# Expert slots in four column quarters instead of two halves in a two-layer hybrid diffusion backbone

## The chip, the cores and the metric

The kernel runs on one core of a Trainium2 chip. The metric is the device time of one execution in microseconds, as the median of three runs. All arithmetic of the part that is changed is in fp32.

## The reference

Two layers, each a mixer (differential attention beside a Mamba-2 scan) and an expert-choice mixture of experts. There are 512 latent rows and 256 context rows of 1024 columns. Only the mixture of experts is touched. Each of 16 experts picks its best rows: 64 latent ones, and in layer 0 also 32 context ones. The second layer has no context output.

```python
def expert_choice_ffn(h, w_router, w_gate, w_up, w_down):
    b, n, d = h.shape
    cap = EC_CAPACITY * n // N_EXPERTS
    aff = jax.nn.softmax(jnp.einsum("bnd,de->ben", h, w_router).astype(jnp.float32), axis=1)
    gate, idx = lax.top_k(aff, cap)
    xe = jax.vmap(lambda hb, ib: hb[ib])(h, idx)
    hid = jax.nn.silu(jnp.einsum("becd,edf->becf", xe, w_gate)) * jnp.einsum("becd,edf->becf", xe, w_up)
    ye = jnp.einsum("becf,efd->becd", hid, w_down) * gate[..., None].astype(h.dtype)
    return jax.vmap(lambda ib, yb: jnp.zeros((n, d), yb.dtype).at[ib.reshape(-1)].add(yb.reshape(-1, d)))(idx, ye)
```

The inner width is 1408, that is 11 blocks of 128. An expert's weights are 8 row blocks (k) of w_gate and w_up, 704 KB each, and 11 blocks of w_down, 512 KB each: 17 MB per expert and layer.

## The kernel before

The method `moe` runs the 16 experts of a layer one after the other. For the latent slots (`lat`, L1489), the chosen rows stand transposed in xeT and are the stationary operand; the weights stream past them. The 64 slots fill half of the array's 128 columns, so two matmuls stand side by side (j = 0, 1), each taking one half of every 128 inner columns. Their result gl has partitions (j, slot) and is held in three tiles of 512, 512 and 384 columns, gate and up side by side. `act` turns each into SiLU(gate) times up (ScalarE's Tanh, then two operations on VectorE), into lh. `turned` (L1537) transposes lh back by matmuls with the identity, into hlt, and ScalarE copies that into hl, where the inner columns lie on the partitions. The down projection yl (L1623) again has two halves, 512 output columns each.

For the context slots of layer 0 (`con`, L1573), 32 slots fill a quarter of the columns, so four matmuls stand side by side. Their result gc goes through `act`, and VectorE transposes it in blocks of 32 by 32 (L1619) into hc. The down projection yc (L1581) has four quarters of 256 output columns.

`add_rows` (L1663, L1664) weighs the result by the gate and by the layer's modulation G2 on VectorE into ys. A DMA issued by POOL adds the rows of ys to xr, xc or out in memory, at the addresses in sidx. A latent row is added in two pieces of 512 columns (2 KB), a context row in four of 256 (1 KB).

The sync engine (SP) issues all weight loads in the order of the program: w_gate and w_up of the 8 k, then the 11 blocks of w_down. There are 9 buffers gw, 8 of a ring rt and 6 wd, so a load waits for the buffer that an earlier matmul frees. Each DMA that adds to xr or out also waits for the one before it on the same tensor. In layer 0, `following` (called at the eighth block of yl) transposes the next expert's rows (xet) and gathers those of the one after. In layer 1, `pick` takes them from SBUF by matmuls (slp, xpk, xet).

A scheduler orders each engine's instructions by its own estimate, except where `manual_schedule` keeps the order of the code. Before, that is the case for TensorE in layer 0's last expert alone.

One fp32 matmul has two records in the trace: 48 matmuls of gl per expert are 96 records.

Of the kernel before, what the change touches and what calls it, by code (L numbers as in the profile page):

```python
# [8 lines left out]
F32 = mybir.dt.float32  # L9
# [133 lines left out]
class Net:  # L143
# [122 lines left out]
    def consts(self, p1):  # L266
# [5 lines left out]
        self.twice = cst.tile([64, P], F32, name="twice")  # L272
# [11 lines left out]
        for j in range(2):  # L284
            self.lds(self.twice[:, 64 * j:64 * j + 64], I["k_ident"][0:64, 0:64])
# [1074 lines left out]
    def route_b(self, l, psp):  # L1360
# [25 lines left out]
        ps = psp.tile([P, 2, NE], F32, tag="tr", name="sgp", bufs=3)  # L1386
        nc.tensor.matmul(ps.rearrange("p i e -> p (i e)"), self.twice, c.rearrange("p i e -> p (i e)"), start=True, stop=True)
        nc.vector.tensor_scalar(self.gate[:, 0], ps[:, 0], 0.5, None, op0=OP.mult)
        for j in range(2):
            h = slice(64 * j, 64 * j + 64)  # L1390
            nc.vector.tensor_scalar(self.sidx[h, 0], ps[h, 1], 2.0, 2.0 * P * na + j, op0=OP.mult, op1=OP.add)
# [10 lines left out]
    def route_d(self, l, psp):  # L1402
# [17 lines left out]
        nc.vector.tensor_scalar(self.gate[:, 1], ps[:, 0], 0.5, None, op0=OP.mult)  # L1420
        nc.vector.tensor_copy(self.sidx[:, 1], ps[:, 1])
# [62 lines left out]
    def lat(self, gl, k, c):  # L1484

        a, b = FB[c]
        for j in range(2):
            w = self.ws[k].rearrange("p u (t j i) -> p j u t i", j=2, i=64)[:, j, :, a:b]
            self.nc.tensor.matmul(gl[c][64 * j:64 * j + 64, 0:LW[c]].rearrange("p (u t i) -> p u t i", u=2, i=64), self.xT[:, k, 0:64],  # L1489
                                  w, start=k == 0, stop=k == KD - 1, skip_group_check=True)  # L1490

    def gl_tiles(self):
        return [self.scp.tile([P, 512], F32, tag="L", name="gl", bufs=3) for _ in LW]

# [7 lines left out]
    def moe_open(self, l):  # L1502
# [3 lines left out]
        self.G2 = [mw.tile([P, 512 >> s], F32, name="G2" + "lc"[s]) for s in range(2 if ctx else 1)]  # L1506
# [3 lines left out]
    def G2_load(self, l, s, o):  # L1510

        m = 2 << s
        w, q = D // m, P // m
        for j in range(m):
            self.ld(o[q * j:q * j + q], self.modd[l, s:s + 1, 5 * D + w * j:5 * D + w * j + w].to_broadcast([q, w]))

    def moe(self, l):
# [4 lines left out]
        dst = [b.rearrange("n (j c) -> (n j) c", c=512 >> i) for i, b in enumerate(base)]  # L1522
        mw, G2 = self.mw, self.G2
        def act(h, g, u, n, tag):
            th = mw.tile([P, n], F32, tag=tag + "th", name="th", bufs=2)
            nc.scalar.activation(th, g, AF.Tanh, scale=0.5)  # L1526
# [3 lines left out]
        def turned(o, h, c):  # L1530

            a, b = FB[c]
            tr = psp.tile([P, 4, 64], F32, tag="tr", name="hlt", bufs=3)
            for t in range(a, b):
                for j in range(2):
                    p = slice(64 * j, 64 * j + 64)
                    nc.tensor.matmul(tr[p, t - a], h[:, 64 * t:64 * t + 64], self.ident[:, p], start=True, stop=True, skip_group_check=True)  # L1537
            nc.scalar.copy(o[:, a:b], tr[:, 0:b - a])

        xe = None  # L1540
        for e in range(NE):
# [19 lines left out]
            hl = mw.tile([P, NF, 64], F32, tag="hl", name="hl", bufs=1)  # L1561
            h = mw.tile([P, 704], F32, tag="lh", name="lh", bufs=1)
# [13 lines left out]
            def down(e, hc, wd):  # L1576

                y = psp.tile([P, 512], F32, tag="acc", name="yc")[:, 0:256]
                for b in range(NF):
                    for j in range(4):  # L1580
                        nc.tensor.matmul(y[32 * j:32 * j + 32], hc[:, b], wd[b][:, 256 * j:256 * j + 256],  # L1581
                                         start=b == 0, stop=b == NF - 1, skip_group_check=True)
                if last:
                    self.tail = lambda: self.add_last(y, e, dst)
                else:
                    self.add_rows(mw, y, 1, e, G2, dst)

            with self.tc.manual_schedule(engines={mybir.EngineType.PE}) if last else contextlib.nullcontext():
                turn = iter(range(KD) if ctx else ())

                def cons(n):
                    for k in itertools.islice(turn, n):
                        con(k)

                KB = KD - 2
                for k in range(0 if early else KB):
                    for c in range(3):
                        self.lat(gl, k, c)
                    cons(not last)
                for c in range(3):  # L1600
                    for k in range(KD if early else KB, KD):
                        self.lat(gl, k, c)
                    n = LW[c] // 2
                    act(h[:, 256 * c:256 * c + n], gl[c][:, 0:n], gl[c][:, n:2 * n], n, f"l{c // 2}")
# [281 lines left out]
```

## Time and profile before

| | us |
|---|---|
| median of 3 runs | 2473.05 (2472.52 to 2476.19) |
| the profiled execution | 2473.73 |
| its span, first to last instruction | 2471.9 |
| TensorE busy (matmuls) | 2262.0, 92% |
| VectorE, ScalarE, POOL busy | 956.8, 669.7, 430.8 |
| layer 0's experts, from the first gl to the last yc | about 560 to 1355 |
| layer 1's experts | about 1819 to 2472 |

The page's first part has the busy times. A busy TensorE need not run at its best rate, so the durations of groups count more than the share. The windows show for any stretch what each engine did, the granted clock of TensorE (1.00 is 2.4 GHz) and the share of the 16 DMA engines; that share can exceed 1 slightly, as packets overlap. The timeline merges equal neighbours: a row says when a group began, how long it ran to the end of its last one, and how many records it has. Matmuls overlap at their ends, so the time that a group takes is read from its start to the next group's start.

### The profile page before, as it was taken

The numbers are of one execution on the slowest core, as the hardware profiler recorded it, in microseconds if no ns is written. First come the engines' busy times: TensorE is split into PE (matmuls) and PEld (weight loads), VectorE is DVE, ScalarE is ACT, GpSimd is POOL, SyncE is SP. The second block draws the span as 40 slices with busy tenths as digits, with TensorE's granted clock in tenths as the row PEclk, the third lists the DMA queues.
The fourth block names the chain that finished last, engine by engine and source line by source line (L and its number), as shares of the span: only waits on it lengthen the run. The fifth ranks groups of instructions, "written<-read, shape, count | busy, mean of one in ns | idle before, by whom it ended". The sixth has DMA issues, their size and how long they took to land.

```text
span 2471.9 us, 39924 instructions
## 1 busy us (share of the span) xinstructions
PE 2262.0 (92%) x15496; PEld 1255.7 (51%) x15496; DVE 956.8 (39%) x2924; ACT 669.7 (27%) x1835; POOL 430.8 (17%) x554
## 2 busy tenths in 40 slices
PE   6898988999999999999998888998979998888887
PEld 4777777774333333333333667787735533333332
DVE  5789588772011101110011888778731010101010
ACT  4344557422112111211111434555311110111110
POOL 4454333000000100010001364433000000000000
PEclk9999999999999999999999999999989999999999
DMA  7223722589999999999995322614699999999998
GB/s 251 84 75 111 254 57 94 193 292 341 401 402 384 360 374 373 355 359 364 377 364 162 102 82 88 207 59 149 226 377 412 412 416 412 416 413 416 412 417 317
DMA packets 230088, 701.73 MB, mean 284 GB/s; under 512 B 30316, under 2 KB 79452, under 8 KB 229900
## 3 DMA queue, kind: packets, MB, share of 16 engines
q1 hardware_dynamic: 220364, 681.69, 71.3%
q0 software_dynamic: 9536, 17.49, 3.6%
q8 instruction: 123, 2.02, 0.3%
q14 instruction: 65, 0.53, 0.1%
HBM read 675.34 MB, written 23.76 MB: 283 GB/s over the span
## 4 chain that ended last, share of the span: by engine, by line
PE 57%; DMA 18%; DVE 16%; issue 4%; ACT 3%; POOL 1%; SPq 0%; POOLq 0%; ACTq 0%; DVEq 0%
PE gl L1489 17%; PE yl L1623 10%; PE gc L1573 7%; DMA gw<-w_up 6%; DMA gw<-w_gate 5%; PE pacc L172 4%; PE yc L1581 4%; PE oacc L172 3%; DMA rt<-w_down 3%; DMA wd<-w_down 2%; PE xacc L172 1%; DVE nm L1798 1%; PE hlt L1537 1%; PE po L1827 1%; DVE G L1076 1%
## 5 line engine op out<-in xcount | busy, mean ns | idle before, releaser
L1489 PE MATMUL gl<-gw,xeT 128*64 128x512 f32 (+1 forms) x3072 | 669.0, 569 | 56.2 <-DMA gw<-w_up 52.2
L1489 PEld LDWEIGHTS gl<-gw,xeT 128*64 128x64 f32 x3072 | 249.2, 138 | 451.2 <-issue 412.5
L1623 PE MATMUL yl<-rt,hl 128*64 128x512 f32 x1020 | 279.8, 599 | 0.2
L1527 DVE SCALAR_TENSOR_TENSOR th<-th,gl 128x256 f32<-128x256 f32 (+1 forms) x96 | 38.1, 397 | 459.7 <-ACT th L1526 459.7
L172 PE MATMUL pacc<-rt,H 128*128 128x384 f32 (+1 forms) x768 | 204.7, 348 | 4.3 <-ACT V L1717 2.0
L1573 PE MATMUL gc<-gw,xeT 128*32 128x352 f32 x2048 | 181.8, 464 | 0.0
L1526 ACT ACTIVATE th<-gl 128x256 f32<-128x256 f32 (+1 forms) x96 | 35.1, 366 | 531.5 <-PE gl L1489 519.1
L1663 DVE SCALAR_TENSOR_TENSOR ys<-yl,gate,G2l 128x512 f32<-128x512 f32 x32 | 24.0, 751 | 375.8 <-PE yl L1623 375.8
L1664 POOL DMA_INDIRECT out<-ys,sidx x16 | 24.8, 1550 | 723.7 <-DVE ys L1663 723.7
L172 PEld LDWEIGHTS pacc<-rt,H 128*128 128x128 f32 x768 | 136.3, 195 | 17.4 <-issue 6.3
L172 PE MATMUL xacc<-H,rt 128*128 128x512 f32 (+1 forms) x448 | 135.8, 379 | 7.1 <-ACT H L803 6.6
L1527 DVE SCALAR_TENSOR_TENSOR th<-th,gc 128x352 f32<-128x352 f32 x16 | 8.3, 520 | 324.0 <-ACT th L1526 324.0
L172 PE MATMUL pacc<-rt,L 128*128 128x384 f32 (+1 forms) x384 | 129.2, 336 | 0.0
L1623 PEld LDWEIGHTS yl<-rt,hl 128*64 128x64 f32 x1020 | 71.6, 136 | 98.6 <-issue 90.8
L1429 POOL DMA_INDIRECT xe<-xn2d,gidx x16 | 15.1, 943 | 610.9 <-PE xet L1439 491.5
L1526 ACT ACTIVATE th<-gc 128x352 f32<-128x352 f32 x16 | 7.4, 463 | 406.8 <-PE gc L1573 406.8
L138 POOL TENSOR_TENSOR rt<-raw,rt 128x384 fp32r<-128x384 f32 (+1 forms) x88 | 100.2, 1163 | 92.0 <-ACT rt L130 90.7
L1573 PEld LDWEIGHTS gc<-gw,xeT 128*32 128x32 f32 x2048 | 57.0, 109 | 106.1 <-issue 102.5
L1623 PE MATMUL yl<-wd,hl 128*64 128x512 f32 x388 | 108.8, 604 | 0.6 <-DMA wd<-w_down 0.5
L172 PE MATMUL oacc<-woh,mT 128*128 128x512 f32 x304 | 107.3, 410 | 0.0
L172 PEld LDWEIGHTS xacc<-H,rt 128*128 128x128 f32 x448 | 82.7, 198 | 22.6 <-ACT H L803 7.4
L1803 ACT ACTIVATE e<-sc,nm,rq 128x768 f32<-128x768 f32 (+1 forms) x80 | 72.0, 903 | 54.3 <-DVE nm L1799 50.1
(411 smaller groups left out, 3643.3 us busy)
## 6 DMA issues: line engine op xcount, KB each, us to landing
gw<-w_gate SPq DMA_DIRECT2D x256, 704.0 KB
gw<-w_up SPq DMA_DIRECT2D x256, 704.0 KB
rt<-w_down SPq DMA_DIRECT2D x255, 512.0 KB
wd<-w_down SPq DMA_DIRECT2D x97, 512.0 KB
mr<-w_mod SPq DMA_DIRECT2D x80, 512.0 KB
raw<-w_in SPq DMA_DIRECT2D x48, 256.0 KB
raw<-w_in SPq DMA_DIRECT2D x64, 192.0 KB
RB<-acsd SPq DMA_DIRECT2D x20, 512.0 KB
```

Source lines behind the costliest of these rows:

```text
L138: e.tensor_tensor(lo.bitcast(F32R), x, hi, op=OP.subtract)
L172: self.nc.tensor.matmul(o, a[x].bitcast(F32R), b[y].bitcast(F32R), start=start and i == 0, stop=stop and i == 2, **kw)
L1076: nc.vector.scalar_tensor_tensor(E[:, h], cbm[:, 1], d[:, 1, h:h + 1], E[:, h], op0=OP.mult, op1=OP.add)
L1489: self.nc.tensor.matmul(gl[c][64 * j:64 * j + 64, 0:LW[c]].rearrange("p (u t i) -> p u t i", u=2, i=64), self.xT[:, k, 0:64], w, start=k = ...
L1526: nc.scalar.activation(th, g, AF.Tanh, scale=0.5)
L1527: nc.vector.scalar_tensor_tensor(th, th, 1.0, g, op0=OP.add, op1=OP.mult)
L1537: nc.tensor.matmul(tr[p, t - a], h[:, 64 * t:64 * t + 64], self.ident[:, p], start=True, stop=True, skip_group_check=True)
L1573: nc.tensor.matmul(gc[u][32 * j:32 * j + 32].rearrange("p (t i) -> p t i", i=32), xT[:, k, 64:96], w, start=k == 0, stop=k == KD - 1, skip ...
L1581: nc.tensor.matmul(y[32 * j:32 * j + 32], hc[:, b], wd[b][:, 256 * j:256 * j + 256], start=b == 0, stop=b == NF - 1, skip_group_check=True)
L1623: nc.tensor.matmul(y[64 * j:64 * j + 64], hl[:, b], wd[b][:, 512 * j:512 * j + 512], start=b == 0, stop=b == NF - 1, skip_group_check=True)
L1664: nc.gpsimd.indirect_dma_start(out=dst[i], out_offset=bass.IndirectOffsetOnAxis(ap=self.sidx[:, i, e:e + 1], axis=0), in_=ys, in_offset=No ...
L1803: nc.scalar.activation(ei[:, 0:w], sc[:, i * w:i * w + w], AF.Exp, scale=rq[:, t, i:i + 1], bias=nm[:, i:i + 1], accum_out=sm[:, i:i + 1])
```

## The change

All slots go in groups of 32. The 64 latent slots are two groups g, and for each group four matmuls stand side by side, one per quarter of the inner (or output) columns. The inner columns of blocks 0 to 7 are one gl tile per group; blocks 8 to 10 of both groups share the third. VectorE transposes h in blocks of 32 by 32, as it did for the context; `turned` and its matmuls are gone. Latent rows are added in four pieces of 256 columns, one DMA per group. The order of TensorE is written out for all experts of layer 0 but the first, and in it yc follows yl from the fifth block on. The gate and address tables get a third column, and are spread over the quarters by eight small matmuls (sgp) instead of one.

```diff
-FB = ((0, 4), (4, 8), (8, 11))
+FA = 8
...
     def lat(self, gl, k, c):
-        a, b = FB[c]
-        for j in range(2):
-            w = self.ws[k].rearrange("p u (t j i) -> p j u t i", j=2, i=64)[:, j, :, a:b]
-            self.nc.tensor.matmul(gl[c][64 * j:64 * j + 64, 0:LW[c]].rearrange("p (u t i) -> p u t i", u=2, i=64), self.xT[:, k, 0:64],
-                                  w, start=k == 0, stop=k == KD - 1, skip_group_check=True)
+        w = self.ws[k].rearrange("p u (t j i) -> p j u t i", j=4, i=32)
+        for g, (a, b), o in (((c, (0, FA), 0),) if c < 2 else ((0, (FA, NF), 0), (1, (FA, NF), 192))):
+            n = 64 * (b - a)
+            for j in range(4):
+                self.nc.tensor.matmul(gl[c][32 * j:32 * j + 32, o:o + n].rearrange("p (u t i) -> p u t i", u=2, i=32),
+                                      self.xT[:, k, 32 * g:32 * g + 32], w[:, j, :, a:b], start=k == o == 0, stop=k == KD - 1,
+                                      skip_group_check=True)
...
-        def turned(o, h, c):
-            a, b = FB[c]
-            tr = psp.tile([P, 4, 64], F32, tag="tr", name="hlt", bufs=3)
-            for t in range(a, b):
-                for j in range(2):
-                    p = slice(64 * j, 64 * j + 64)
-                    nc.tensor.matmul(tr[p, t - a], h[:, 64 * t:64 * t + 64], self.ident[:, p], start=True, stop=True, skip_group_check=True)
-            nc.scalar.copy(o[:, a:b], tr[:, 0:b - a])
+        def down(y, h, wd, b, new=True):
+            for j in range(4):
+                nc.tensor.matmul(y[32 * j:32 * j + 32], h[:, b], wd[b][:, 256 * j:256 * j + 256],
+                                 start=new and b == 0, stop=b == NF - 1, skip_group_check=True)
...
+            def lat_act(c):
+                if c < 2:
+                    act(h[:, c, 0:256], gl[c][:, 0:256], gl[c][:, 256:512], 256, "l0")
+                    nc.vector.transpose(hl[:, c, 0:FA].rearrange("p t s -> p (t s)"), h[:, c, 0:256])
+                    return
+                v = gl[2][:, 0:384].rearrange("p (x u i) -> p x u i", x=2, u=2)
+                act(h[:, :, 256:FQ], v[:, :, 0], v[:, :, 1], 192, "l2")
+                for g in range(2):
+                    nc.vector.transpose(hl[:, g, FA:NF].rearrange("p t s -> p (t s)"), h[:, g, 256:FQ])
...
-            with self.tc.manual_schedule(engines={mybir.EngineType.PE}) if last else contextlib.nullcontext():
+            with self.tc.manual_schedule(engines={mybir.EngineType.PE}) if ctx and e else contextlib.nullcontext():
...
-                turned(hl, h, 0)
-                cons(not last)
-                turned(hl, h, 1)
+                if ctx and not last:
+                    for k in range(0 if early else KB, KD):
+                        con(k)
+                    yc = con_act()
                 y = self.scp.tile([P, 512], F32, tag="L", name="yl", bufs=3)
                 for b in range(NF):
-                    if b == 4:
-                        turned(hl, h, 2)
-                        if ctx and not last:
-                            act(h2, gc[0], gc[1], FQ, "c")
-                            nc.vector.transpose(hc.rearrange("p t s -> p (t s)"), h2)
+                    for g in range(2):
+                        down(y[:, 256 * g:256 * g + 256], hl[:, g], wd, b, g == 0)
+                    if ctx and not last and b > 3:
+                        for i in range(5) if b == 4 else (b,):
+                            down(yc, hc, wd, i)
                     if b == 7 and e + 1 < NE:
                         xe = self.following(l, e, xe, nt)
-                    for j in range(2):
-                        nc.tensor.matmul(y[64 * j:64 * j + 64], hl[:, b], wd[b][:, 512 * j:512 * j + 512],
-                                         start=b == 0, stop=b == NF - 1, skip_group_check=True)
-                self.add_rows(mw, y, 0, e, G2, dst)
+                for g in range(2):
+                    self.add_rows(mw, y[:, 256 * g:256 * g + 256], g, e, G2[0], dst[0])
...
-        ys = mw.tile([P, 512 >> i], F32, tag=f"ys{i}", name="ys", bufs=2)
+        ys = mw.tile([P, 256], F32, tag="ys", name="ys", bufs=4)
```

TensorE's order in layer 0 from the end of an expert's main loop, before (the fifteenth expert; gl and gc are the projections, hlt the transposes, yl and yc the down projections, xet the next expert's rows):

```order
L1489 MATMUL gl<-gw,xeT 64x512 x4
L1489 MATMUL gl<-gw,xeT 64x384 x2
L1573 MATMUL gc<-gw,xeT 32x352 x8
L1489 MATMUL gl<-gw,xeT 64x512 x4
L1489 MATMUL gl<-gw,xeT 64x384 x2
L1537 MATMUL hlt<-ident,lh 64x64 x8
L1573 MATMUL gc<-gw,xeT 32x352 x4
L1537 MATMUL hlt<-ident,lh 64x64 x8
L1623 MATMUL yl<-rt,hl 64x512 x8
L1537 MATMUL hlt<-ident,lh 64x64 x6
```

The same place of the changed kernel:

```order
L1490 MATMUL gl<-gw,xeT 32x512 x8
L1490 MATMUL gl<-gw,xeT 32x192 x8
L1573 MATMUL gc<-gw,xeT 32x352 x8
L1490 MATMUL gl<-gw,xeT 32x512 x16
L1490 MATMUL gl<-gw,xeT 32x192 x16
L1573 MATMUL gc<-gw,xeT 32x352 x16
L1536 MATMUL yl<-rt,hl 32x256 x40
L1536 MATMUL yc<-rt,hc 32x256 x20
```

Before, gl is 64 columns wide and gc 32, and hlt stands ahead of yl; now every matmul here is 32 wide, and gl's last two k, gc's last two and five blocks of yl follow each other with nothing between.

TensorE's order in the down projection of the same expert, before:

```order
L1623 MATMUL yl<-rt,hl 64x512 x2
L1439 MATMUL xet<-ident,xe 128x96 x5
L1623 MATMUL yl<-rt,hl 64x512 x2
L1439 MATMUL xet<-ident,xe 128x96 x3
L1581 MATMUL yc<-rt,hc 32x256
L1623 MATMUL yl<-rt,hl 64x512 x2
L1581 MATMUL yc<-rt,hc 32x256 x8
L1623 MATMUL yl<-rt,hl 64x512 x2
L1581 MATMUL yc<-rt,hc 32x256 x4
```

And of the changed kernel:

```order
L1536 MATMUL yl<-rt,hl 32x256 x8
L1536 MATMUL yc<-rt,hc 32x256 x4
L1438 MATMUL xet<-ident,xe 128x96 x8
L1536 MATMUL yl<-wd,hl 32x256 x8
L1536 MATMUL yc<-wd,hc 32x256 x4
```

Before, yl, xet and yc are mixed in pieces that are no whole groups; now whole blocks of yl and yc alternate, and xet stands in one piece.

POOL's order in layer 0 with the semaphores that each instruction waits for, before (xr and xc are the adds of latent and context rows, xe the gather; DMASW are the landings of POOL's own DMAs):

```order
L1664 DMA xr<-ys,sidx_6128 1024x512 [waits DMASW7_49,DVE_49]
L1664 DMA xc<-ys,sidx_6128 1024x256 [waits DMASW0_49,DVE_49]
L1429 DMA xe<-xn2d,gidx_6126 96x1024 [waits DMASW1_49,PE_49]
L1664 DMA xr<-ys,sidx_6128 1024x512 [waits DMASW2_49,DVE_49]
L1664 DMA xc<-ys,sidx_6128 1024x256 [waits DMASW3_49,DVE_49]
```

And of the changed kernel:

```order
L1666 DMA xr<-ys,sidx_6125 2048x256 [waits DMASW0_49,DVE_49]
L1666 DMA xc<-ys,sidx_6125 1024x256 [waits DMASW7_49,DVE_49]
L1666 DMA xr<-ys,sidx_6125 2048x256 [waits DMASW2_49]
L1428 DMA xe<-xn2d,gidx_6123 96x1024 [waits DMASW1_49,PE_49]
L1666 DMA xr<-ys,sidx_6125 2048x256 [waits DMASW4_49,DVE_49]
```

An expert now has two adds to xr, and the second waits for the landing of the first; the gather stands behind it. In layer 1 the 32 adds to out stand in a row, each waiting for the landing of the one before.

## Rows read from the trace of the kernel before

**Rows 1.** Windows: stretch, length, busy time of PE, PEld, DVE, ACT, POOL, granted clock, DMA share, GB/s.

```profile
600.00:647.30 47.30, 47.30 (x410) 17.41 (x408) 5.13 (x12) 7.21 (x23) 4.08 (x3) 1.00 1.03 404
890.97:940.87 49.90, 49.90 (x410) 16.82 (x408) 5.11 (x11) 7.24 (x23) 4.07 (x3) 1.00 0.95 366
2000.00:2472.00 472.00, 403.01 (x2227) 162.29 (x2223) 44.40 (x117) 54.31 (x156) 16.98 (x11) 0.97 0.99 401
```

**Rows 2.** Chain that ended last, in order of time: start, length in us, what.

```profile
599.92 3.44 PE yl L1623 x16
...
1290.17 3.44 PE yl L1623 x16
...
2082.03 14.85 DMA gw<-w_gate
```

**Rows 3.** Timeline of TensorE, a late expert of layer 0: start, length, instruction, records.

```profile
802.86 1.06 PE L1581 MATMUL yc<-rt,hc 128*32 128x256 f32 x12
803.85 1.08 PE L1623 MATMUL yl<-wd,hl 128*64 128x512 f32 x4
...
809.73 2.58 PE L1489 MATMUL gl<-gw,xeT 128*64 128x512 f32 x12
812.25 1.39 PE L1573 MATMUL gc<-gw,xeT 128*32 128x352 f32 x16
813.57 2.58 PE L1489 MATMUL gl<-gw,xeT 128*64 128x512 f32 x12
```

**Rows 4.** Timeline of TensorE, the last expert of layer 0.

```profile
1308.14 19.11 PE L1489 MATMUL gl<-gw,xeT 128*64 128x512 f32 x96
1327.09 1.10 PE L1537 MATMUL hlt<-ident,lh 128*64 128x64 f32 x32
1328.25 3.65 PE L1623 MATMUL yl<-rt,hl 128*64 128x512 f32 x16
```

**Rows 5.** Timeline of TensorE, the first expert of layer 0.

```profile
589.12 8.49 PE L1573 MATMUL gc<-gw,xeT 128*32 128x352 f32 x112
597.53 0.45 PE L1537 MATMUL hlt<-ident,lh 128*64 128x64 f32 x6
...
610.60 3.66 PE L1581 MATMUL yc<-rt,hc 128*32 128x256 f32 x64
614.08 1.48 PE L1581 MATMUL yc<-wd,hc 128*32 128x256 f32 x24
```

**Rows 6.** Timeline of TensorE, modulation at the kernel's start.

```profile
25.02 1.96 PE L363 MATMUL macc<-mw,sC 128*32 128x128 f32 x64
```

**Rows 7.** Timeline of SP's DMA issues, first w_gate of two successive experts.

```profile
628.14 0.33 SPq L155 DMA_DIRECT2D gw<-w_gate  x1
...
672.90 0.33 SPq L155 DMA_DIRECT2D gw<-w_gate  x1
```

**Rows 8.** Timeline of VectorE, layer 0.

```profile
1137.97 0.42 DVE L1528 TENSOR_TENSOR lh<-th,gl 128x256 f32<-128x256 f32 x1
...
1140.48 0.55 DVE L1619 STREAM_TRANSPOSE hc<-ch 128x352 f32<-128x352 f32 x1
```

**Rows 9.** The tile ys: instructions, durations in ns min/median/max, first and last start.

```profile
L1663 DVE SCALAR_TENSOR_TENSOR ys<-yc,gate,G2c x2: 484/484/484, 809.4 to 859.3; 128x256 f32<-128x256 f32 x2
```

**Rows 10.** Timelines of VectorE, POOL, SP and TensorE, end of layer 0.

```profile
1338.31 0.75 DVE L1663 SCALAR_TENSOR_TENSOR ys<-yl,gate,G2l 128x512 f32<-128x512 f32 x1 [9.90 <-PE yl L1623]
...
1339.34 1.55 POOL L1664 DMA_INDIRECT xr<-ys,sidx  x1 [28.64 <-DVE ys L1663]
...
1344.37 1.86 SPq L155 DMA_DIRECT2D xin<-xr  x4
...
1365.05 2.82 PE L859 MATMUL trx<-ident,xin 128*128 128x128 f32 x12 [10.39 <-ACT xin L851]
```

**Rows 11.** DMA issues, 1330 to 1380: count, median us from issue to landing.

```profile
xc<-rt,sidx POOLq DMA_INDIRECT x1, 4.8
```

**Rows 12.** DMA queues (packets, MB, share of 16 engines), 2041 to 2053, then 1107 to 1122.

```profile
q0 software_dynamic: 144, 0.26, 11.8%
...
q0 software_dynamic: 288, 0.39, 15.0%
```

More of the change, by code (lines that the diff above doesn't have):

```diff
@@ L1385, in route_b @@
         yield STEP
[L1386 to L1391 removed]
+        ps = psp.tile([P, 2, 2, NE], F32, tag="tr", name="sgp", bufs=3)
+        for g in range(2):
+            for j in range(4):
+                nc.tensor.matmul(ps[32 * j:32 * j + 32, g].rearrange("p i e -> p (i e)"), self.ident[0:64, 32 * g:32 * g + 32],
+                                 c.rearrange("p i e -> p (i e)"), start=True, stop=True, skip_group_check=True)
+        nc.vector.tensor_scalar(self.gate[:, 0:2], ps[:, :, 0], 0.5, None, op0=OP.mult)
+        for j in range(4):
+            h = slice(32 * j, 32 * j + 32)
+            nc.vector.tensor_scalar(self.sidx[h, 0:2], ps[h, :, 1], 4.0, 4.0 * P * na + j, op0=OP.mult, op1=OP.add)
         if l == 0:
@@ L1505, in moe_open @@
         self.wp = self.tc.alloc_tile_pool(name=f"wd{l}", bufs=1, reuse_waits="tile", side="right")
-        self.G2 = [mw.tile([P, 512 >> s], F32, name="G2" + "lc"[s]) for s in range(2 if ctx else 1)]
+        self.G2 = [mw.tile([P, 256], F32, name="G2" + "lc"[s]) for s in range(2 if ctx else 1)]
         for s in range(2 if ctx else 1):
@@ L1510, in G2_load @@
     def G2_load(self, l, s, o):
[L1512 to L1515, printed above, removed]
+        for j in range(4):
+            self.ld(o[32 * j:32 * j + 32], self.modd[l, s:s + 1, 5 * D + 256 * j:5 * D + 256 * j + 256].to_broadcast([32, 256]))
     def moe(self, l):
@@ L1574, in con, with con_act @@
                                          start=k == 0, stop=k == KD - 1, skip_group_check=True)
[L1576 to L1581, printed above, removed]
-                                         start=b == 0, stop=b == NF - 1, skip_group_check=True)
[L1583 to L1586, printed above, removed]
-            with self.tc.manual_schedule(engines={mybir.EngineType.PE}) if last else contextlib.nullcontext():
[L1589 to L1593, printed above, removed]
+            def con_act():
+                th = mw.tile([P, FQ], F32, tag="cth", name="th", bufs=2)
+                nc.scalar.activation(th, gc[0], AF.Tanh, scale=0.5)
+                nc.vector.scalar_tensor_tensor(th, th, 1.0, gc[0], op0=OP.add, op1=OP.mult)
+                nc.vector.tensor_tensor(h2, th, gc[1], op=OP.mult)
+                nc.vector.transpose(hc.rearrange("p t s -> p (t s)"), h2)
+                return psp.tile([P, 512], F32, tag="acc", name="yc")[:, 0:256]
+            def lat_act(c):
[8 more added lines that the diff above has]
+            with self.tc.manual_schedule(engines={mybir.EngineType.PE}) if ctx and e else contextlib.nullcontext():
                 KB = KD - 2
+                both = ctx and not early and not last
                 for k in range(0 if early else KB):
@@ L1598, in moe @@
                         self.lat(gl, k, c)
-                    cons(not last)
+                    if both:
+                        con(k)
                 for c in range(3):
@@ L1602, in moe @@
                         self.lat(gl, k, c)
[L1603 to L1604 removed]
+                    lat_act(c)
                 if early:
```

53 lines of the change are left out of this document (27 added, 26 removed).

## The prediction

> **What bounds the kernel now.** I read the windows by expert first. In layer 0 one expert takes 47.3 us early and 49.90 us later; TensorE is busy for all of it at a granted clock of 1.00, and DMA is at 1.03 of its engines early, 0.95 later [rows 1]. So TensorE sets the pace there, but with DMA close behind: faster TensorE will meet it. In layer 1 DMA is at 0.99 and TensorE at 403 of 472 us [rows 1], and the chain of waits runs from one weight transfer to the next [rows 2]. Time that TensorE saves there is worth nothing.
>
> Then TensorE's timeline, for what a layer 0 expert is made of. One k of the main loop (the latent slots' gl, then the context slots' gc) takes 813.57 - 809.73 = 3.84 us [rows 3]. Alone, gl runs 8 k in 1327.09 - 1308.14 = 18.95 us, 2.37 per k [rows 4], and gc runs 7 k (112 records) in 597.53 - 589.12 = 8.41 us, 1.20 per k [rows 5]. Side by side they cost 3.84 - 3.57 = 0.27 us more. What differs is the shape: gl uses the array in halves of 64 columns, gc in quarters of 32, and the order changes from one to the other twice per k. So a change of shape costs about 0.135 us, 2.2 us in 8 k.
>
> Late experts cost another 49.9 - 47.3 = 2.6 us because the scheduler breaks yc into the middle of yl. There 12 yc records take 803.85 - 802.86 = 0.99 us, 83 ns each [rows 3]; unbroken, 64 take 614.08 - 610.60 = 3.48 us, 54 ns each [rows 5].
>
> **The change part by part.** *Halves become quarters.* gl goes from 6 matmuls per k to 16, yl from 22 per expert to 88, with the same column-time: four quarters of half the width per pair. Now gl, gc, yl and yc have one shape, so the 2.2 us of shape changes should go; only the few around xet stay, as now. Bounds: 0 to 2.2; I take 2.2, since gl alone and gc alone, the nearest rows, both run without the surcharge. Quarters are slightly dearer per column: gc's 8.41 us over 14 x 352 columns is 1.71 ns, gl's 18.95 over 11,264 is 1.68 [rows 4, 5], so gl pays 0.3 us. The narrow quarters of 192 lie between gc's 352 and those of 128 in the first stage, where 64 records took 1.96 us [rows 6]: 0.245 per group of eight records against 0.218 by gc's column rate. At most 0.03 us for each of 32 such groups bounds this from above at 1.0 us. yl by quarters of 256 costs what yc does, 3.48/8 = 0.435 per group [rows 5]; two make the 0.87 of a half pair, so nothing.
>
> *Transposes move to VectorE.* 44 hlt records leave TensorE: 32 of them took 1328.25 - 1327.09 = 1.16 us [rows 4], so 1.6 us per expert. VectorE gets four transposes per expert. One of 352 columns took 0.55 us, a product of 256 columns 0.42 [rows 8]. Cover: in layer 0 two gc steps (2.4 us) stand between the last gl and the first yl, and the chain behind the last gl is only needed at its ninth block. hc's chain, four operations of about the length of rows 8, some 2.5 us, has five yl blocks, 4.3 us, ahead of yc. So nothing on the path. In layer 1 that cover is missing: yl may wait for one product, about 0.4 us, less than the hlt that goes, and DMA hides it.
>
> *TensorE's order is written out in layer 0 after the first expert.* yc follows whole groups of yl, so the 2.6 us of the late experts go.
>
> TensorE's expert is then 47.3 - 2.2 + 0.3 - 1.6 = 43.8 us. DMA does not follow: between the first w_gate issues of two successive experts, while DMA was saturated, lie 672.90 - 628.14 = 44.76 us [rows 7]. I take 44.8 as the new period. Bounds: 43.8, and 0.95 x 49.9 / 1.03 = 46.0 by the shares of rows 1. From the first expert's yl at 599.92 to the fifteenth's at 1290.17 are 14 periods, 690.3 us [rows 2]: 14 x 44.8 = 627.2, **-63.1**. In the first expert the hlt ahead of yl goes: **-1.2**. In the rest of the fifteenth and in the sixteenth TensorE saves 2.6 + 1.2; with DMA behind it I count **-1.5** (0 to -3.8).
>
> *Result rows in two adds.* Each add to xr or out waits for the one before to land, and now there are two per expert. In mid-layer nothing waits for it: behind the waiting add POOL's queue has the next gather, which is needed an expert later. At the end of layer 0 it counts: the add was issued at 1339.34, VectorE having begun at 1338.31, and the sync engine, held until it landed, issued the next layer's first load at 1344.37; that reaches TensorE at 1365.05 after 10.4 us of idle [rows 10]. Before: 0.75 + 0.28 + 5.0 = 6.0 us. Now 0.48 for a piece of 256 columns [rows 9] + 0.28 + 5.0 + 4.9: pieces of half the size land no sooner, 4.8 us [rows 11]. That is 10.7 us, **+4.7**, and the same at the kernel's end, **+4.7**. Bounds for the two: +3 (the second overlaps its issue) to +17 (a busy DMA).
>
> The Trainium skill ("DMA: Bandwidth & Descriptors", Anatomy of one DMA) gives a transfer by this path a fixed part of some 2.0 us. Rows 11 show more than twice that for an add. By the page's figure each end would lose about 2 us, and the sum below would be some 5 us lower.
>
> *Small pieces in layer 1.* An add in 2 KB pieces took 11.8% of 16 engines x 12 us = 22.7 us. With the context's 1 KB add beside it, 15.0% of 16 x 15 = 36.0, so 13.3 for the latter [rows 12]. Two of 13.3 instead of 22.7 are 4 us over 16 engines, 0.25 us per expert; 16 experts: **+4.0** (0 to 6). *Layer 1's start*: eight small sgp matmuls and an early pick stand ahead of gl, which frees the first buffers: **+0.5**.
>
> Sum: -63.1 - 1.2 - 1.5 + 4.7 + 4.7 + 4.0 + 0.5 = -51.9. The profiled execution took 2473.73 us (2471.9 of span), 0.7 above the median: 2421.8, or **2421 us** against the median.
>
> **The rivals.**
> *The surcharge stays*, because it comes from alternating two operands, not from the shape. For it: no row shows two operands of one shape alternating. Against it: gl alone alternates three accumulators and 16 weight sets at no surcharge [rows 4]. The expert is then 46.0 on TensorE: 14 x 46.0 = 644, 46.3 saved, in place of 63.1: 2438.
>
> *DMA falls further behind than 44.8.* Its share reached 1.03 with 404 GB/s [rows 1]; a steady 46.0 gives the same 2438.
>
> *Each added matmul pays for its issue: slower.* Per expert 92 matmuls become 216, 248 more records. If every one cost the 28 ns by which broken yc records exceed whole ones (83 - 54), the expert would be 43.8 + 6.9 = 50.7: 14 x 50.7 = 710, +19.5, and with +13.9 from the adds and layer 1 some 2507. It decides from about 20 ns per record. Against it: the narrow quarters of rows 6 run at 31 ns per record in all.
>
> The Trainium skill ("TensorEngine Tiling (Array Packing)", Instruction Overhead) charges about 60 cycles per matmul, so that smaller tiles pay more often. At 2.4 GHz that would be 25 ns for 124 matmuls, an estimate of 3.1 us per expert and 2451 in all. Rows 6 do not bear that out for matmuls that lie side by side.
>
> *The change does little*: new waits at yc or xet as long as what goes. Nothing in layer 0's queues is late by the rows above: 2470.
>
> **How the numbers follow.** Forecast 60%, its own range 2409 to 2433. Surcharge stays 12%; DMA slower 12%; issue cost, at any size, 8%, half of it past the break-even; little change 3%; better (TensorE's 43.8 holds and the tail overlaps, 2403) 5%. The range 2405 to 2445 leaves out about 2 in 10. Faster by over 0.2% (what a measurement of this kernel can tell from no change) 0.93, within it 0.03, slower 0.04.
>
> **What would show it.** Right: layer 0 experts 44 to 45.5 us apart at a DMA share near 1.0; one k of gl and gc in about 3.6 us; no hlt; TensorE waiting a little for weights; two adds some 5 us apart at both ends. Wrong: 3.8 us per k (the surcharge stayed), gl groups longer than gc's column rate (issue), waits for VectorE ahead of yl or yc, or a DMA share well under 1 at 46 us and more.

## The result, and the profile after

| | before | after |
|---|---|---|
| median, us | 2473.48 (2472.52 to 2476.19) | 2430.96 (2429.14 to 2438.21) |
| profiled execution, its span | 2473.73, 2471.9 | 2429.65, 2427.9 |

The ratio is 0.983 (95% interval 0.981 to 0.985). The forecast was 2421: faster was right, and the time lies in the range 2405 to 2445, but between the two profiled executions 44.1 us went where 51.9 were forecast.

TensorE did what the forecast said. One k of the main loop in the changed kernel's timeline (start, duration, and the number of records at the end):

```profile
882.13 2.55 PE L1490 MATMUL gl<-gw,xeT 128*32 128x512 f32 x32
884.50 1.37 PE L1573 MATMUL gc<-gw,xeT 128*32 128x352 f32 x16
885.68 2.55 PE L1490 MATMUL gl<-gw,xeT 128*32 128x512 f32 x32
```

From gl to gl are 885.68 - 882.13 = 3.55 us, where [rows 3] had 3.84. That is gl alone (2.37) and gc alone (1.18) with nothing on top: two operands still alternate, now in one shape, so the surcharge belonged to the change of shape and is gone, and nothing is paid for 248 more records. The Trainium skill ("TensorEngine Tiling (Array Packing)", Key Properties) says that a change of tiling mode drains TensorE. The trace fits that, at 0.14 us a change here.

VectorE's product of the result rows marks each expert's end. Its rows in layer 0 after:

```profile
614.08 0.47 DVE L1665 SCALAR_TENSOR_TENSOR ys<-yc,gate,G2c 128x256 f32<-128x256 f32 x1
...
656.88 0.88 DVE L1665 SCALAR_TENSOR_TENSOR ys<-yl,gate,G2l 128x256 f32<-128x256 f32 x2 [13.13 <-PE yl L1536]
...
700.48 0.88 DVE L1665 SCALAR_TENSOR_TENSOR ys<-yl,gate,G2l 128x256 f32<-128x256 f32 x2 [13.14 <-PE yl L1536]
...
918.73 0.88 DVE L1665 SCALAR_TENSOR_TENSOR ys<-yl,gate,G2l 128x256 f32<-128x256 f32 x2 [13.14 <-PE yl L1536]
...
964.43 0.88 DVE L1665 SCALAR_TENSOR_TENSOR ys<-yl,gate,G2l 128x256 f32<-128x256 f32 x2 [13.14 <-PE yl L1536]
...
1241.54 0.88 DVE L1665 SCALAR_TENSOR_TENSOR ys<-yl,gate,G2l 128x256 f32<-128x256 f32 x2 [13.13 <-PE yl L1536]
1242.34 0.47 DVE L1665 SCALAR_TENSOR_TENSOR ys<-yc,gate,G2c 128x256 f32<-128x256 f32 x1
...
1278.59 0.88 DVE L1665 SCALAR_TENSOR_TENSOR ys<-yl,gate,G2l 128x256 f32<-128x256 f32 x2 [8.29 <-PE yl L1536]
```

The same products of the context rows in the kernel before:

```profile
615.63 0.48 DVE L1663 SCALAR_TENSOR_TENSOR ys<-yc,gate,G2c 128x256 f32<-128x256 f32 x1 [4.16 <-PE yc L1581]
...
1308.38 0.48 DVE L1663 SCALAR_TENSOR_TENSOR ys<-yc,gate,G2c 128x256 f32<-128x256 f32 x1 [1.66 <-PE yc L1581]
```

Read the intervals. Early experts are 700.48 - 656.88 = 43.60 us apart: TensorE's own pace (43.8 forecast), no wait for weights. From the eighth expert on it is 45.7 (964.43 - 918.73), and (1241.54 - 918.73) / 7 = 46.1 in the mean up to the fifteenth: now the weights set the pace. The waits after 870 us (total, times, longest) and the windows (busy of PE, PEld, DVE, ACT, POOL, granted clock, DMA share, GB/s) show it:

```profile
PE gl L1490 <- DMA gw<-w_up: 17.2, 10, 2.4
PE yl L1536 <- DVE hl L1587: 0.2, 1, 0.2
```

```profile
635.00:860.00 225.00, 225.00 (x3380) 111.39 (x3376) 35.94 (x91) 32.55 (x104) 28.10 (x20) 1.00 1.03 400
900.00:1250.00 350.00, 337.38 (x5040) 179.54 (x5036) 50.78 (x126) 49.22 (x159) 42.47 (x30) 0.99 1.03 397
1950.00:2350.00 400.00, 345.61 (x4430) 146.84 (x4426) 48.45 (x148) 38.59 (x117) 30.84 (x20) 0.99 1.03 410
```

In the last expert of layer 0 TensorE waits three times for w_up, 4.7 us in all. Behind the third wait its granted clock is 0.50, the lower of its two levels (1.2 GHz):

```profile
1262.06 6.59 PE L1490 MATMUL gl<-gw,xeT 128*32 128x512 f32 x56 [2.40 <-DMA gw<-w_up]
```

```profile
1262.00:1266.00 4.00, 3.94 (x20) 1.15 (x24) 1.29 (x3) 0.38 (x1) 0.00 (x0) 0.50 0.91 347
```

Both ends now have two adds, one behind the other. POOL at the end of layer 0, the sync engine's load that waits for them, and the kernel's end:

```profile
1279.53 1.57 POOL L1666 DMA_INDIRECT xr<-ys,sidx  x1 [27.19 <-DVE ys L1665]
1284.15 1.56 POOL L1666 DMA_INDIRECT xr<-ys,sidx  x1 [3.05 <-issue]
```

```profile
1288.17 1.75 SPq L154 DMA_DIRECT2D xin<-xr  x4
```

```profile
2412.99 0.87 DVE L1665 SCALAR_TENSOR_TENSOR ys<-yl,gate,G2l 128x256 f32<-128x256 f32 x2 [11.14 <-PE yl L1536]
2413.75 1.54 POOL L1666 DMA_INDIRECT out<-ys,sidx  x1 [33.37 <-DVE ys L1665]
2418.38 1.54 POOL L1666 DMA_INDIRECT out<-ys,sidx  x1 [3.09 <-DMA out<-ys,sidx]
```

The second add starts 4.6 us after the first at both. The kernel's end before, with one add:

```profile
2461.64 0.75 DVE L1663 SCALAR_TENSOR_TENSOR ys<-yl,gate,G2l 128x512 f32<-128x512 f32 x1 [11.47 <-PE yl L1623]
```

From VectorE's start to the next layer's load are 1288.17 - 1278.59 = 9.6 us, where [rows 10] had 1344.37 - 1338.31 = 6.1.

The page's DMA queues (packets, MB, share) show one thing more, after:

```profile
q0 software_dynamic: 14080, 17.46, 3.9%
q8 instruction: 185, 3.03, 0.5%
```

Before, q8 had 123 packets. In all runs q8 has one packet for 126 or 127 of TensorE's matmul records, so I take it for their queue: the added matmuls have to be fetched, by the same DMA engines that bring the weights.

For layer 1, and for experiments, I use one more number, the **weight period**: the mean interval between the landings of an expert's last gate or up packet, from the packets in the trace; in layer 0 over the last 14 intervals, in layer 1 over the last 11. The last column says whether the ring of buffers for w_down, and with it most weight buffers, starts off a multiple of 256 bytes in a partition; it matters from e7 on.

| kernel | median | layer 0 | layer 1 | q8 packets | buffers off 256 B |
|---|---|---|---|---|---|
| before | 2473.5 | 48.24 | 42.65 | 123 | no |
| changed | 2431.0 | 45.86 | 43.23 | 185 | no |
| e1 order alone | 2440.6 | 46.60 | 42.68 | 123 | no |
| e2 add split | 2492.3 | 48.39 | 43.29 | 123 | yes |
| e3 halves in layer 1 | 2420.5 | 45.90 | 42.67 | 154 | no |
| e4 quarters, little context | 2417.1 | 45.53 | 43.24 | 163 | no |
| e5 halves, little context | 2396.7 | 44.94 | 42.55 | 100 | no |
| e6 more instructions | 2659.5 | 46.57 | 57.5 | 154 | yes |
| e7 halves last and in layer 1 | 2436.2 | 46.42 | 43.32 | 152 | yes |
| e8 quarters, no order | 2510.6 | 50.04 | 43.23 | 185 | no |
| e9 as e7, aligned | 2414.5 | 45.92 | 42.68 | 152 | no |
| e10 changed + 128 B | 2446.9 | 46.41 | 43.64 | 185 | yes |
| e11 changed + 256 B | 2428.8 | 45.86 | 43.24 | 185 | no |
| e12 as e9, more matmuls | 2419.1 | 45.85 | 42.88 | 170 | no |

### The profile page after: what moved, and what is told of

Read it like the earlier page. It is cut to its first block, busy times and chain, and to the rows that moved or that the text cites. A ratio compares the mean times of both kernels' runs of the same rounds, so it can differ in the third digit from the quotient of the medians.

```text
span 2427.9 us, 55950 instructions
## 1 busy us (share of the span) xinstructions
PE 2175.3 (90%) x23460; PEld 1335.8 (55%) x23460; DVE 995.3 (41%) x3088; ACT 635.9 (26%) x1739; POOL 480.9 (20%) x584
## 5 line engine op out<-in xcount | busy, mean ns | idle before, releaser
L1490 PE MATMUL gl<-gw,xeT 128*32 128x512 f32 (+1 forms) x8192 | 655.6, 466 | 62.9 <-DMA gw<-w_up 62.7
L1490 PEld LDWEIGHTS gl<-gw,xeT 128*32 128x32 f32 x8192 | 277.7, 111 | 441.9 <-issue 404.3
L1536 PE MATMUL yl<-rt,hl 128*32 128x256 f32 x4080 | 247.5, 380 | 13.6 <-PE gl L1490 9.2
L1536 PEld LDWEIGHTS yl<-rt,hl 128*32 128x32 f32 x4080 | 134.1, 110 | 117.8 <-issue 16.0
L1666 POOL DMA_INDIRECT out<-ys,sidx x32 | 49.5, 1546 | 710.7 <-DVE ys L1665 599.1
L1665 DVE SCALAR_TENSOR_TENSOR ys<-yl,gate,G2l 128x256 f32<-128x256 f32 x64 | 28.0, 479 | 361.3 <-PE yl L1536 361.3
L1443 ACT ACTIVATE xeT<-xet,MC,A 128x64 f32<-128x64 f32 (+1 forms) x256 | 74.3, 424 | 169.2 <-PE xet L1438 169.2
L1536 PE MATMUL yl<-wd,hl 128*32 128x256 f32 x1552 | 101.4, 382 | 4.4 <-DMA wd<-w_down 3.8
L1573 PEld LDWEIGHTS gc<-gw,xeT 128*32 128x32 f32 x2048 | 68.6, 110 | 56.2 <-issue 43.9
L1666 POOL DMA_INDIRECT xr<-ys,sidx x32 | 49.9, 1560 | 194.9 <-DVE ys L1665 109.1
```

Source lines behind the costliest of these rows:

```text
L1443: nc.scalar.activation(xT[:, kk, c:d], tr[:, k, c - a:d - a], AF.Identity, scale=self.A2[:, s, kk:kk + 1], bias=self.MC[:, l, s, 24 + kk:2 ...
L1490: self.nc.tensor.matmul(gl[c][32 * j:32 * j + 32, o:o + n].rearrange("p (u t i) -> p u t i", u=2, i=32), self.xT[:, k, 32 * g:32 * g + 32] ...
L1536: nc.tensor.matmul(y[32 * j:32 * j + 32], h[:, b], wd[b][:, 256 * j:256 * j + 256], start=new and b == 0, stop=b == NF - 1, skip_group_che ...
L1573: nc.tensor.matmul(gc[u][32 * j:32 * j + 32].rearrange("p (t i) -> p t i", i=32), xT[:, k, 64:96], w, start=k == 0, stop=k == KD - 1, skip ...
L1665: nc.vector.scalar_tensor_tensor(ys, y, self.gate[:, i, e:e + 1], G2, op0=OP.mult, op1=OP.mult)
L1666: nc.gpsimd.indirect_dma_start(out=dst, out_offset=bass.IndirectOffsetOnAxis(ap=self.sidx[:, i, e:e + 1], axis=0), in_=ys, in_offset=None, ...
```

## The experiments

**e1: the order alone.** The kernel before, with

```diff
-with self.tc.manual_schedule(engines={mybir.EngineType.PE}) if last else contextlib.nullcontext():
+with self.tc.manual_schedule(engines={mybir.EngineType.PE}) if ctx and e else contextlib.nullcontext():
```

> The kernel before with one thing of the change: TensorE takes every layer-0 expert but the first in the order of the code (the context rows' last product after the slots' last product), where before only the last expert was written out. Halves, turns on TensorE and one add stay. Theory of the forecast: the late experts lose 2.6 us each to the broken order, and all of it comes back, so the 14 periods go from 690.3 us to 14 x 47.3 = 662 and the time to about 2445 us; the DMA share of the core stays below 1.00 in layer 0. Rival: the order cost nothing by itself, TensorE was simply full, 2470 to 2475 us.

2440.55 us, ratio 0.987 (0.985 to 0.988), near the theory's 2445. VectorE's products of the slots, every one 47.39 us after the last up to the fifteenth expert:

```profile
606.32 0.75 DVE L1663 SCALAR_TENSOR_TENSOR ys<-yl,gate,G2l 128x512 f32<-128x512 f32 x1 [9.72 <-PE yl L1623]
...
653.71 0.75 DVE L1663 SCALAR_TENSOR_TENSOR ys<-yl,gate,G2l 128x512 f32<-128x512 f32 x1 [9.72 <-PE yl L1623]
...
1269.73 0.75 DVE L1663 SCALAR_TENSOR_TENSOR ys<-yl,gate,G2l 128x512 f32<-128x512 f32 x1 [9.72 <-PE yl L1623]
```

The DMA share is 1.01 and 0.99 in the two stretches of layer 0, not under 1.00 in both as expected. So the order alone is worth 35.0 us of span (2471.9 to 2436.9), most of the change's 44.0. Everything else brings 9.0: up to the load of the next layer's rows it brings 1310.73 - 1288.17 = 22.6 us, of which the rest of the kernel gives 13.6 back.

**e2: the add in two.** The kernel before, with

```diff
-ys = mw.tile([P, 512 >> i], F32, tag=f"ys{i}", name="ys", bufs=2)
+for g in range(2 - i):
+    ys = mw.tile([P, 256], F32, tag="ys", name="ys", bufs=4)
 ...
+    nc.gpsimd.indirect_dma_start(out=dst[i], out_offset=bass.IndirectOffsetOnAxis(ap=self.sidx[:, i + 2 * g, e:e + 1], axis=0),
```

> The kernel before with one thing of the change: the slots' result rows of an expert go out in two adds of 1 KB pieces (the columns cut in two), not one of 2 KB pieces. Halves stay. Theory A, the pieces are what makes the weights of layer 1 come 0.6 us later per expert (42.65 before, 43.24 in the changed kernel): the layer-1 period becomes 43.2, and with the second add's wait at the end of both layers (about 3.5 and 4.7 us) the time is 2473.5 + 9 + 8 = 2490 us. Theory B, instruction fetches or the quarters slow the weights, and the pieces only add their packet time (128 x (2 x 101 - 176) ns over 16 engines = 0.2 us): period 42.9, 2473.5 + 3 + 8 = 2485 us.

2492.26 us, ratio 1.007 (1.005 to 1.008); weight period 43.29 in layer 1. It looked like theory A. It isn't: e7, with one whole add in layer 1 and the same addresses of these buffers, has 43.32. What slowed the weights of both is the addresses (e10); the pieces cost nothing that this pair shows. Their packets do fill the 16 DMA engines for longer, 1.64 us an expert in e2 and 1.42 in e7, but the weights come no later for it.

**e3: halves in layer 1.** The changed kernel with both ways of cutting an expert, and

```diff
+def quarters(l, e):
+    return l == 0
```

> The changed kernel with quarters in layer 0 alone; layer 1 has the halves, the turns on TensorE and the one add of before. Theory: layer 1 is paced by its weights, so the halves cost it nothing there; the period goes back from 43.24 to 42.65 us (15 x 0.6 = 9 us) and the second add's wait at the end (4.65 us) goes, 2431 - 13.7 = 2417 us. Rival: the slower weights of layer 1 come from something else than quarters and adds, then only the end comes back, 2426 us. If TensorE's halves bind in layer 1 after all, 2431 or more.

2420.46 us, ratio 0.978 (0.976 to 0.979); layer 1's period is back at 42.67 and the end at one add. Confirmed within 4 us.

**e4 and e5: how fast can the weights come?** The context products of layer 0 cut to one step, with quarters and with halves (both with the order); the context rows' results are incomplete in both. For instance

```diff
-for k in range(0 if early else KB, KD):
+for k in (KD - 1,):
     con(k)
```

> The changed kernel with the context rows' products of layer 0 cut to one of 8 steps and one of 11 steps for all experts but the last (their results are left incomplete); loads, gathers, adds and turns stay. Theory A, the DMA itself needs 45.9 us for an expert of layer 0: the period stays 45.9 and the time 2428 to 2432 us, with TensorE's busy time down by about 10 us per expert. Theory B, TensorE's work beside it (its reading of the same memory, or its late release of weight buffers) holds the weights back: the period falls to 44.8 or less, 14 x 1.1 = 15 us, 2415 us.

> The kernel of the first experiment (halves, order written out) with the context rows' products of layer 0 cut in the same way as in the fourth, so that TensorE doesn't bind and the period is what the DMA of the kernel before needs. Theory A: the forecast took one period of before (44.76 us) where periods alternate; the mean of the first five of before is 45.2 us, so the DMA floor of the halves is 45.2 us, 0.3 us under the 45.53 of the quarters in the fourth experiment; time about 2400 us. Theory B: the floor of before was 44.76 as forecast and the change itself slows the weights by 0.8 us or more: period 44.8 or less, about 2394 us.

Layer 0's window in e4 and in e5:

```profile
900.00:1250.00 350.00, 274.10 (x3652) 135.88 (x3644) 48.98 (x125) 49.21 (x159) 44.03 (x31) 0.94 1.03 399
```

```profile
900.00:1250.00 350.00, 284.38 (x1628) 104.33 (x1630) 37.98 (x82) 55.93 (x179) 31.59 (x23) 0.93 1.02 401
```

TensorE idles a fifth of the time and the weights still need 45.53 us with quarters (theory A of e4, though 0.33 under the changed kernel) and 44.94 with halves, nearer to theory B of e5. So [rows 7] (44.76) was a fair sample of the halves' floor, and the quarters themselves add 0.59, as in layer 1 (43.23 against 42.67). The time of e4, 2417 us, is that of its theory B, but by another way: the first expert's context products are gone too, and the first interval between landings is 47.6 us, not 52.3.

**e6: more instructions on VectorE.** e3 and, in each layer-1 expert but the last,

```diff
+for _ in range(256 if l and e + 1 < NE else 0):
+    nc.vector.tensor_copy(tiny, ys[0:1, 0:1])
```

> The kernel of the third experiment (halves in layer 1) with 256 copies of one number on VectorE in each layer-1 expert but the last, which nothing waits for: only the instruction fetches of layer 1 rise, from about 1.6 packets of 16 KB for an expert towards the 3.9 of the quarters. Theory A, fetches are most of the 0.6 us by which the quarters slow the weights of layer 1: the period goes from 42.67 to 43.1 or more, 2420.5 + 7 = 2427 us. Theory B, the two adds are most of it: the period stays within 0.1 of 42.67, 2420 to 2422 us.

2659.46 us, and the run settles nothing about fetches. The copies took 141 ns each as recorded and more from one to the next, so VectorE filled the expert and held TensorE up; layer 1's experts came 58 us apart:

```profile
L1696 DVE COPY tiny<-ys 1x1 f32<-1x1 f32 x1830 | 258.4, 141 | 60.0
```

Nor did q8 rise (154 packets, as in e3); another queue did, from 66 to 96 packets. q8 is not the queue of VectorE's instructions.

**e7: halves for the last layer-0 expert too**, that is `return l == 0 and e < NE - 1`.

> The kernel of the third experiment, with halves and one add for the last expert of layer 0 as well. The changed kernel takes 9.6 us from VectorE's first product to the reading of the next layer's rows, before took 6.06. Theory: the second add's wait of 3.5 us goes and up to 1.6 us of turns on TensorE come, a gain of 2 to 3.5 us over the third experiment, 2417 to 2418.5 us. Rival: TensorE's halves are late enough at the last expert that nothing is gained, 2420 us or more.

2436.17 us, ratio 0.985 (0.983 to 0.986): 16 us slower than e3, which neither view foresaw. Layer 1 has e3's code and one add, but its weights come more slowly. The window in e3, then in e7:

```profile
1950.00:2350.00 400.00, 349.66 (x1912) 142.32 (x1908) 37.19 (x99) 47.07 (x135) 13.88 (x9) 0.98 1.02 414
```

```profile
1950.00:2350.00 400.00, 345.00 (x1892) 139.54 (x1890) 37.92 (x100) 46.92 (x135) 15.43 (x10) 0.98 1.02 408
```

The same DMA share moves 408, not 414 GB/s. What differs is the layout: 128 bytes more of tables a partition than in e3 shift the buffers behind them, the ring of w_down and eight of the nine gate and up buffers. The first buffer of the ring starts at byte 22,784 of a partition before (89 x 256), at 22,528 in the changed kernel (88 x 256), at 22,912 in e2 and e7, 22,848 in e6.

**e8: quarters without the order**, e1's line the other way round.

> The changed kernel with TensorE's order in layer 0 left to the scheduler, as before, but for the last expert. Theory: a late expert lost 2.6 us to the broken order when TensorE was full; with quarters TensorE has 2.1 us to spare (43.8 of 45.9), so the order costs only the rest, 0.5 us x 14, and more at the end of layer 0: 2436 to 2440 us. Rival A: the scheduler breaks nothing in the quarters, 2431 us. Rival B: it breaks as much as in the halves and the slack doesn't cover it, 2455 us or more.

2510.63 us, ratio 1.014 (1.012 to 1.015): slower than before; rival B, at a price far over its own. TensorE's waits from 900 to 1250 us, and one of them in its timeline:

```profile
PE xet L1438 <- DMA xe<-xn2d,gidx: 55.4, 6, 9.6
```

```profile
1019.87 1.37 PE L1573 MATMUL gc<-gw,xeT 128*32 128x352 f32 x16
1030.81 0.87 PE L1438 MATMUL xet<-ident,xe 96*128 96x96 f32 x4 [9.57 <-DMA xe<-xn2d,gidx]
```

The scheduler put the turn of the gathered rows (xet) into the next expert's loop, where TensorE stood 9.6 us for a gather. No slack of 2 us covers that. So the two parts of the change don't add: the order is worth 35 us with the halves and 80 with the quarters.

**e9, e10, e11: the place of the buffers.** e9 is e7 with 128 bytes fewer of tables (its extra columns lie in unused places); e10 and e11 are the changed kernel with an unused table:

```diff
+self.pad = cst.tile([P, 32], F32, name="pad")      # e10; [P, 64] in e11
+nc.gpsimd.memset(self.pad, 0.0)
```

> The kernel of the seventh experiment with 128 bytes a partition less of tables: the index and gate columns of the last layer-0 expert stand where its quarters would have had theirs. With this the weight buffers of the left side start at multiples of 256 bytes in a partition again, as in all kernels so far with a layer-1 base period of 42.3 to 42.4 us (before, the changed kernel, the first, third, fourth, fifth and eighth experiment); the three with 42.9 (the second, sixth and seventh) all start off them. Theory A, the place of the buffers makes the DMA slower: the layer-1 mean goes back from 43.32 to 42.67 us, layer 0 from 46.4 to 45.9, and the time from 2436 to 2417 us. Theory B, it is something else in the program or its loading: 2434 to 2439 us again, or no relation to the address.

> The changed kernel with an unused table of 128 bytes a partition ahead of the weight buffers, which start 128 bytes off a multiple of 256 with it. Theory A, the place of the buffers: the layer-1 mean goes from 43.23 to about 43.9 us, the layer-0 period from 45.86 to 46.4, and the time to 2431 + 17 = 2448 us. Theory B, something else: 2431 us, periods as in the changed kernel.

> The changed kernel with an unused table of 256 bytes a partition at the same place: the control of the tenth experiment, the buffers start at multiples of 256 again. Theory A: 2431 us and the periods of the changed kernel (45.86 and 43.23 us). Theory B: the same as the tenth, whatever that is.

e9: 2414.53 us, ratio 0.977 (0.975 to 0.978). e10: 2446.89, ratio 0.989 (0.987 to 0.990). e11: 2428.82, ratio 0.981 (0.980 to 0.983). All three as theory A has it. Layer 1's window in e10 and e11:

```profile
1950.00:2350.00 400.00, 344.52 (x4406) 144.98 (x4398) 48.42 (x148) 38.81 (x117) 30.80 (x20) 0.99 1.03 406
```

```profile
1950.00:2350.00 400.00, 344.41 (x4424) 146.21 (x4415) 48.45 (x148) 38.79 (x117) 30.82 (x20) 1.00 1.03 410
```

An unused table of 128 bytes costs 16 us, one of 256 nothing. The mean packet of 5632 bytes takes 218.9 ns in e10's window, 217.0 in e11's. The median is 215 in both; 31% of these packets take 220 ns or more in e10, 9% in e11. The Trainium skill ("DMA: Bandwidth & Descriptors", How a descriptor splits into AXI transactions) says that a read which doesn't begin at a multiple of 256 bytes is started at the one below it. If the side that is written went by the same rule, one transaction more in 22 would be 4.5% for every packet, an estimate from the page. Measured are 0.9% in the mean and nothing at the median, so the runs show the loss but not that it comes this way.

e9 is the fastest of the kernels that do all the work: 16.4 us under the changed one. From the last weight packet of layer 0 to the next layer's load it takes 1281.91 - 1272.5 = 9.4 us, e3 1288.80 - 1277.3 = 11.5: 2.1 less, the low end of the 2 to 3.5 expected of e7. The medians are 5.9 us apart; the rest isn't accounted for.

**e12: more matmuls in layer 1.** e9, with

```diff
+for u in range(2):
+    self.nc.tensor.matmul(v[:, u], self.xT[:, k, 0:64], w[:, u], start=k == u == 0, stop=k == KD - 1, skip_group_check=True)
```

and yl cut in the same way.

> The kernel of the ninth experiment (halves and one add in layer 1, period 42.68 us) with TensorE's products of layer 1 cut in two along the moved columns: 70 more products for an expert (gl 48 to 96, yl 22 to 44), the same columns in all; the quarters have 124 more. Adds, loads and buffers are as in the ninth. Theory A, the fetching of TensorE's instructions is what slows the weights under the quarters (3.9 packets of 16 KB an expert, not 1.6, and 0.57 us): about 2.9 packets an expert and a layer-1 mean of 42.9 to 43.1 us, 2414.5 + 5 = 2419 us. Theory B, it is the pieces of the adds or the quarters' way through the array: 42.68 us again, 2413 to 2416 us. If TensorE's idle share in layer 1 falls under 2%, it binds and the run tells nothing.

2419.13 us, ratio 0.979 (0.977 to 0.980). Layer 1's period is 42.88 (42.68 in e9), with 18 more q8 packets, adds and buffers the same, and TensorE idle for 5.6% of the window:

```profile
1950.00:2350.00 400.00, 377.76 (x3326) 283.52 (x3322) 36.92 (x101) 49.94 (x145) 15.42 (x10) 1.00 1.02 413
```

The same window in e9, and the waits for gate and up weights of e9 and of e12 from 2050 to 2390 us:

```profile
1950.00:2350.00 400.00, 350.91 (x1958) 144.08 (x1956) 39.50 (x105) 48.76 (x140) 13.87 (x9) 0.98 1.02 415
```

```profile
PE gl L1518 <- DMA gw<-w_up: 38.1, 34, 2.3
```

```profile
PE gl L1524 <- DMA gw<-w_up: 2.7, 12, 0.3
```

So more instructions on TensorE do slow the weights: 0.20 us an expert, at 18 more packets in 16 experts. It is theory A's sign, a little under its range, but not yet its cause. By their own time on the engines (945 ns each) the packets explain 0.07 of the 0.20. Most of the rest lies in the weights' packets, which take longer (216.4 ns for 5632 bytes, 216.0 in e9). The cut also adds weight loads on TensorE (PEld, the second count: 3322 for 1956), and no run tells their reading of the memory from the fetches. TensorE itself is close to its bound in e12: it hardly waits for weights any more, though the DMA share is the same 1.02. The quarters fetch 31 packets more than e3 in layer 1; if all of it goes with the packets, that is 0.34 of their 0.56 us. Where the other 0.2 comes from stays open.

## Why the prediction was right, and where it missed

- **TensorE's expert, 43.8.** Right: 43.60. The changes of shape gave 8 x 0.29 = 2.3 us (2.2 forecast), and hlt is gone. The rivals "the surcharge stays" and "issue cost" are out by the 3.55 us per k.
- **The 14 periods, -63.1.** Between the first and the fifteenth expert's yc products lie 692.75 us before and 628.26 after: -64.5. But 44.8 was no pace that anything kept: seven intervals are TensorE's 43.6 to 43.9, on weights that the DMA had brought ahead, and the other seven are the DMA's, 46.1 in the mean. The mean came out right by luck, because the lead happened to last half the layer. The rival "DMA falls further behind", with 46.0, describes the second half.
- **The first expert, -1.2.** Its yc product comes 1.55 us earlier. Right.
- **The rest of the fifteenth and the sixteenth, -1.5 (0 to -3.8).** This step failed. From the fifteenth's yc product to the last yl product are 1278.59 - 1242.34 = 36.25 us, 29.93 before: +6.3. I took TensorE's time for an expert whose weights are late. Its last gate and up packets landed at 1261.5; before, they landed at 1297.7, 10 us before TensorE began this expert at all. So TensorE waited 4.7 us for w_up in this expert, and the clock at 0.50 behind the last wait cost it some 2.5 us more: six groups of four 512-column records start 0.85 us apart there, 0.43 at full clock. When the bound moves to the DMA, the end of the stage is the last landing plus what follows, and here what follows ran slowly as well.
- **DMA's pace, 44.8 (43.8 to 46.0).** Late in the layer 45.9, near the upper bound. [rows 7] was fair for halves (44.94 in e5); the quarters add 0.59 (e4) and the context's products 0.33 more. That more instructions on TensorE slow the weights, which the forecast put at nothing, is a part of that (e12, in layer 1); whether by their fetches or by TensorE's weight loads stays open.
- **The second add, +4.7 at each end.** At the kernel's end 14.87 us from VectorE's product, 10.22 before: +4.6 (+5.2 from the last gate and up landing on). At the end of layer 0 it is +3.5. Together that is inside the bounds. That pieces of half the size land no sooner was wrong: the new adds landed 3.8 and 3.9 us after issue, the one add of before 4.7 and 4.9. The fixed 2.0 us of the Trainium skill ("DMA: Bandwidth & Descriptors", Anatomy of one DMA) is not what these adds take: 4.6 us lie between two of which the second waits for the first.
- **Small pieces in layer 1, +4.0.** The size was off: from the first to the last landing of layer 1 are 650.4 us, 643.0 before, +7.4. And the reason: the packets of the adds took 0.22 us more an expert, near the 0.25 priced, but e2 beside e7 shows that this costs no time, and e12 that more instructions on TensorE do.
- **The order, 2.6 us for a late expert.** Right: 49.90 became 47.39 (e1). Its share of the whole is larger than forecast, 35 of the 44 us, because the quarters give back behind the 14 periods much of what they gain in them. e8 shows that the quarters without it lose.
- **Transposes on VectorE, nothing on the path.** Right in layer 0: yl waited 0.2 us for hl in all after 870 us, and never before. In layer 1, from 2050 to 2390 us, it waited 0.9 us an expert for gl and hl, beside 5.4 that gl waited for weights.

By stages the forecast was too good by 6.1 us in layer 0 (-59.7, not -65.8), too bad by 1.2 at its end, too good by 2.9 in layer 1 and by 0.5 at the kernel's end, too bad by 0.4 between the layers. Together that is the 7.8 us missing.

## What to carry to other kernels

When an engine close to a second bound is made faster, take the lead of the one over the other into the sum: the new pace holds only until the lead is spent, and the stage ends with the slower one's last delivery. Do one part alone before crediting the whole; here a line of order did four fifths of it, and without that line the rest loses. When code is compared in which DMA binds, keep the buffers' addresses at the same multiple, or a table of 128 bytes decides the comparison.

## What the runs showed of the hardware

- Weight buffers that start off a multiple of 256 bytes in a partition made the weights come 0.9 to 1.5% more slowly: 43.64 against 43.24 us an expert, 16 to 18 us in the kernel (e10 against the changed kernel and e11), and again in e7 and e9 (43.32 and 42.68, 21.6 us). That 256 is the unit, and not 512 less something, rests on starts of 0 and 256 modulo 512 (full rate) and 128, 320 and 384 (lower rate; 320 in e6's layer 0 alone, 46.57 against 45.90 in e3). One in nine of the gate and up buffers and three in eleven of w_down's start off a multiple of 256 in every kernel; aligning these too wasn't tried.
- TensorE's instructions come through a DMA queue of their own in 16 KB packets of some 0.95 us: 123 for 15,496 matmul records before, 185 for 23,460 after. More of them cost the weights time: 0.20 us an expert with 1.1 packets more (e12), 0.07 of it the packets themselves.
- Adds of 1 KB pieces to rows at addresses landed 3.8 to 3.9 us after issue, adds of 2 KB pieces 4.7 to 4.9, at the two ends, where the weights had already landed.
- Behind three waits for weights (0.7, 1.6 and 2.4 us) TensorE's granted clock was 0.50, 1.2 GHz, from 1262 to 1266 us of the changed kernel.
- The turn of shape between halves and quarters of the array costs TensorE 0.14 us: 3.84 us per k with two such turns, 3.55 without.
